# One block of loads re-cut for the DMA engines, first stores held back, first pair turned early: a weight-normalised matrix product on one Trainium2 core

## Chip, cores, metric

One core of a Trainium2 chip. The metric is the device time of one execution in microseconds; times are medians of several runs. A run is "fast" or "slow" by its time against the fastest run of the same kernel; comparisons use fast runs. A ratio below is the mean time of one kernel's fast runs over the mean of the other's of the same rounds, so it is not quite the ratio of the medians that stand beside it.

## The reference

```python
W_adapted = W + scale * (lora_A @ lora_B)                       # 256 x 256
W_norm = np.sqrt(np.sum(W_adapted ** 2, axis=0, keepdims=True) + 1e-8)
W_final = W_adapted / W_norm * m
y = x.reshape(-1, 256) @ W_final                                # 32768 x 256, float32
```

Nearly all bytes are x (33.6 MB in) and y (33.6 MB out).

## The kernel before

x comes in eight blocks of 4096 rows. A block lies in SBUF as 128 partitions of 32 KB, one contiguous stretch of DRAM for each partition. There are five block buffers; y is written over x in the same buffer and stored from there, so the load of block 5 waits for the store of block 0, and so on. A block is eight chunks, two chunks are a pair. For each pair GpSimd rounds x to bf16, TensorE turns it (transposes), VectorE copies it out of PSUM, TensorE multiplies, ScalarE copies the product back.

```python
def load_x(n):
    nc.sync.dma_start(out=in_sbuf(*parts[n]), in_=in_dram(x_flat, *parts[n])
    ).then_inc(sem(f"load{n}"), 16)

def store_y(n):
    nc.scalar.dma_start(out=in_dram(out_flat, *parts[n]), in_=in_sbuf(*parts[n])
    ).then_inc(sem(f"store{n}"), 16)
# ... lora_A, lora_B, m on ScalarE's queue; W and all of x on SyncE's
for n in range(len(parts)):
    b = parts[n][0] // CH
    if b >= XBUFS and parts[n][0] % CH == 0:
        nc.sync.wait_ge(sem(f"store{b - XBUFS}"), 16)
    load_x(n)
# ... ScalarE, after chunk g
    n = part_of[g]
    if g == NCH - 1 or part_of[g + 1] != n:      # the block's last chunk
        nc.scalar.drain().then_inc(sem("done"), 1)
        nc.scalar.wait_ge(sem("done"), n + 1)
        store_y(n)
# ... TensorE
    nc.tensor.wait_ge(dv, 8)                     # the weights are ready
    nc.tensor.sem_inc(sem("room"), 2)
    turned(0)
    with nc.Fori(0, NPR // 2, 1, engines=[PE], head_slot={PE: 128}):
        turned(1)
        product(0)
        product(1)
        turned(0)
```

Of the kernel before, what the change touches and what calls it, by code (L numbers as in the profile page):

```python
# [11 lines left out]
def kernel(  # L12
# [10 lines left out]
    nc = tc.nc  # L23
    P = 128
# [5 lines left out]
    x_flat = x.flatten_outer_dims()  # L30
    out_flat = out.flatten_outer_dims()
    N, IN = x_flat.shape
    OUT = W.shape[1]
    R = lora_A.shape[1]
    KC = IN // P
    J = 4
    DJ = 32
    BLK = DJ * P
    NBLK = N // BLK
# [3 lines left out]
    XBUFS = 5  # L43
    CH = DJ // J
    NCH = NBLK * CH

    NPR = NCH // 2
    PRB = CH // 2
    NXB = 2
    NXT = 2  # L50
    F8 = 2 * J * P

# [7 lines left out]
    def sb(name, shape, dtype):  # L60
        return ctx.enter_context(nc.sbuf_tensor(name, shape, dtype))
# [4 lines left out]
    x_bufs = [sb(f"x_sb{k}", [P, DJ, IN], FP32) for k in range(XBUFS)]  # L66
    xb_bufs = [sb(f"xb{k}", [P, 2 * J, IN], BF16) for k in range(NXB)]
    xt_bufs = [sb(f"xt{k}", [P, F8, KC], BF16) for k in range(NXT)]
    w_nat = sb("w_nat", [P, KC, OUT], FP32)
    a_nat = sb("a_nat", [P, KC, R], FP32)  # L70
    b_nat = sb("b_nat", [R, OUT], FP32)
# [28 lines left out]
    def sem(name):  # L100
        if name not in sems:
            sems[name] = tc.alloc_semaphore(name)
        return sems[name]
# [1 line left out]



    parts = [(b * CH, CH) for b in range(NBLK - 1)]
    parts += [(NCH - CH, CH // 2), (NCH - CH // 2, CH // 2)]
    part_of = {}  # L110
    for n, (g0, cnt) in enumerate(parts):
        for g in range(g0, g0 + cnt):
            part_of[g] = n

    def in_sbuf(g0, cnt):
        b, c = divmod(g0, CH)
        return x_bufs[b % XBUFS][:, c * J : (c + cnt) * J, :]

    def in_dram(dram, g0, cnt):
        return dram[g0 * J * P : (g0 + cnt) * J * P].rearrange("(p j) k -> p j k", p=P)  # L120

    def load_x(n):
        nc.sync.dma_start(
            out=in_sbuf(*parts[n]), in_=in_dram(x_flat, *parts[n])
        ).then_inc(sem(f"load{n}"), 16)

    def store_y(n):
        nc.scalar.dma_start(
            out=in_dram(out_flat, *parts[n]), in_=in_sbuf(*parts[n])
        ).then_inc(sem(f"store{n}"), 16)  # L130


# [1 line left out]
        out=w_nat[:], in_=W.rearrange("(p t) o -> p t o", t=KC)  # L134
    ).then_inc(sem("load_w"), 16)
    nc.scalar.dma_start(
        out=a_nat[:], in_=lora_A.rearrange("(p t) r -> p t r", t=KC)
    ).then_inc(sem("load_a"), 16)
    nc.scalar.dma_start(out=b_nat[:], in_=lora_B).then_inc(sem("load_b"), 16)
    nc.scalar.dma_start(out=m_row[:], in_=m[None, :]).then_inc(sem("load_m"), 16)  # L140
    for n in range(len(parts)):
        b = parts[n][0] // CH
        if b >= XBUFS and parts[n][0] % CH == 0:
            nc.sync.wait_ge(sem(f"store{b - XBUFS}"), 16)
        load_x(n)


    nc.gpsimd.memset(zeros[:], 0.0).then_inc(sem("pool"), 1)
    nc.gpsimd.wait_ge(sem("pool"), 1)
    nc.gpsimd.affine_select(  # L150
        out=identity[:],
        in_=zeros[:],
# [5 lines left out]
    ).then_inc(sem("ident"), 1)  # L158
    for p in range(NPR):
        b, c = divmod(p, PRB)  # L160
        if p == 0 or part_of[2 * p - 1] != part_of[2 * p]:
            nc.gpsimd.wait_ge(sem(f"load{part_of[2 * p]}"), 16)
        if p >= NXB:
            nc.gpsimd.wait_ge(sem("turned"), p - NXB + 1)
        nc.gpsimd.tensor_copy(  # L165
            out=xb_bufs[p % NXB][:],
            in_=x_bufs[b % XBUFS][:, 2 * c * J : 2 * (c + 1) * J, :],
        ).then_inc(sem("rounded"), 1)

    nc.gpsimd.wait_ge(sem("turned"), NPR - NXB + 1)  # L170
    nc.gpsimd.memset(xb_bufs[NPR % NXB][:], 0.0).then_inc(sem("rounded"), 1)  # L171


    dv = sem("dve")
    nc.vector.memset(ones[:], 1.0)
    nc.vector.memset(eps_col[:], 1e-8).then_inc(dv, 1)
    nc.vector.wait_ge(sem("load_b"), 16)
    nc.vector.tensor_copy(out=b_bf[:], in_=b_nat[:])  # L178
    nc.vector.wait_ge(sem("pe"), 1)
    nc.vector.tensor_copy(out=aT[:], in_=aT_ps).then_inc(dv, 1)  # L180
# [3 lines left out]
        out=wa[:], in0=ab_ps, scalar=float(scale), in1=w_nat[:], op0=ALU.mult, op1=ALU.add  # L184
# [15 lines left out]
    for p in range(NPR):  # L200
        nc.vector.wait_ge(sem("turned"), p + 1)
        nc.vector.tensor_copy(  # L202
            out=xt_bufs[p % NXT][:].rearrange("p r t -> p (r t)").bitcast(FP32),
            in_=xt_ps[p % 2][:],
# [8 lines left out]
        out=norm[:], in_=n2_ps, func=AF.Sqrt, bias=eps_col[:]  # L213
    ).then_inc(sem("act"), 1)
    for g in range(NCH):
        b, c = divmod(g, CH)
        nc.scalar.wait_ge(sem("product"), g + 1)

        nc.scalar.copy(  # L219
            out=x_bufs[b % XBUFS][:, c * J : (c + 1) * J, :], in_=y_ps[g % 2][:]  # L220
        ).then_inc(sem("room"), 1)
        n = part_of[g]
        if g == NCH - 1 or part_of[g + 1] != n:
            nc.scalar.drain().then_inc(sem("done"), 1)
            nc.scalar.wait_ge(sem("done"), n + 1)
            store_y(n)


    pe = sem("pe")
# [17 lines left out]
    i.then_inc(pe, 1)  # L247
    nc.tensor.wait_ge(sem("load_m"), 16)
    nc.tensor.matmul(mb_ps, ones[0:1, :], m_row[:], start=True, stop=True).then_inc(pe, 1)  # L249

    nc.tensor.wait_ge(dv, 8)
    nc.tensor.sem_inc(sem("room"), 2)

    def take(name):

        nc.tensor.sem_inc(sem(name), -1).wait_op(sem(name), 1, "sem-ge")  # L256
# [6 lines left out]
    def turned(p):  # L263
        take("rounded")

        for j in range(2 * J):
            i = nc.tensor.transpose(  # L267
                xt_ps[p % 2][:, j * P : (j + 1) * P],
                xb_bufs[p % NXB][:, j, :].bitcast(FP32),
                identity[:],  # L270
            )
        i.then_inc(sem("turned"), 1)

    def product(p):
        take("copied")
        for h in range(2):
            take("room")
            for t in range(KC):
                for j in j_order:
                    r = (h * J + j) * P  # L280
                    i = nc.tensor.matmul(  # L281
                        y_ps[h][:, j, :],
                        xt_bufs[p % NXT][:, r : r + P, t],
                        w_final[:, t, :],
                        start=(t == 0 and (j % (J // 2)) == 0),
                        stop=(t == KC - 1 and (j % (J // 2)) == (J // 2) - 1),
                    )
            i.then_inc(sem("product"), 1)

    turned(0)  # L290
    with nc.Fori(0, NPR // 2, 1, engines=[PE], head_slot={PE: 128}):
        turned(1)
        product(0)
        product(1)
        turned(0)


    critical.close()
# [40 lines left out]
```

## Time and profile before

| | before |
|---|---|
| median of the first three runs | 164.03 us (163.66 to 164.14) |
| span of the profiled run | 163.2 us |
| share of the 16 DMA engines, both queues | 96.8% |
| busiest compute engine (TensorE) | 65% |
| end of the last packet: 15 engines / the last engine | 159.5 to 160.3 / 162.69 us |

Two kinds of reading occur below. Views of the profile give shares and GB/s of a stretch; they count a packet where it starts, so a short stretch is rough. The packet records of the trace give start, duration, size and queue of every DMA packet, but no engine number; a packet often starts within 3 to 4 ns of the end of another, and such a row of packets (a lane) is read as one engine's. A "count" is one of the 16 landings that the trace has for a DMA's semaphore, read as one for each engine (block 0 of the kernel before: 13.50 to 13.78 us; its last store: 159.84 to 163.16 us). "Lost" time is what a stretch of packets falls short of 433 GB/s, the rate from 60 to 137 us of the kernel before. The lines themselves stand in the prediction.

### The profile page before, as it was taken

The numbers are of one execution on the slowest core, as the hardware profiler recorded it, in microseconds if no ns is written. First come the engines' busy times: TensorE is split into PE (matmuls) and PEld (weight loads), VectorE is DVE, ScalarE is ACT, GpSimd is POOL, SyncE is SP. The second block draws the span as 40 slices with busy tenths as digits, with TensorE's granted clock in tenths as the row PEclk, the third lists the DMA queues.
The fourth block names the chain that finished last, engine by engine and source line by source line (L and its number), as shares of the span: only waits on it lengthen the run. The fifth ranks groups of instructions, "written<-read, shape, count | busy, mean of one in ns | idle before, by whom it ended". The sixth has DMA issues, their size and how long they took to land. (4 is left out here: it accounts for less than half of the span.)

```text
span 163.2 us, 1988 instructions
## 1 busy us (share of the span) xinstructions
PE 105.3 (65%) x786; PEld 85.2 (52%) x786; DVE 47.2 (29%) x44; ACT 63.8 (39%) x67; POOL 62.5 (38%) x39
## 2 busy tenths in 40 slices
PE   1270599789789897898981998619988820892000
PEld 0130577677577775776760867418676610771000
DVE  0429452350532514405230325005051400330000
ACT  3010027548366384473754053900738440062000
POOL 1006381753935738268004940069209003900000
PEclk9999999999999999999998589985899996599755
DMA  5998998998999999999999999999999999998991
GB/s 201 402 498 386 426 474 385 482 418 265 466 426 426 442 410 466 426 394 482 418 426 442 420 426 458 402 458 410 446 414 454 414 446 422 450 442 377 442 430 60
DMA packets 2915, 67.41 MB, mean 413 GB/s; under 512 B 465, under 2 KB 482, under 8 KB 610
## 3 DMA queue, kind: packets, MB, share of 16 engines
q1 hardware_dynamic: 1440, 33.82, 49.0%
q10 hardware_dynamic: 1474, 33.59, 47.8%
q14 instruction: 1, 0.01, 0.0%
HBM read 33.85 MB, written 33.55 MB: 413 GB/s over the span
## 5 line engine op out<-in xcount | busy, mean ns | idle before, releaser
L219 ACT COPY x_sb<-y_ps 128x1024 f32<-128x1024 f32 x64 | 61.9, 1014 | 75.8 <-PE y_ps L281 75.8
L165 POOL CAST xb<-x_sb 128x2048 bf16<-128x2048 f32 x32 | 60.0, 1902 | 79.3 <-DMA x_sb<-in_x_dram 56.0
L281 PE MATMUL y_ps<-w_final,xt 128*128 128x256 bf16 x512 | 64.6, 280 | 12.8 <-PEq L256 12.8
L202 DVE COPY xt<-xt_ps 128x1024 f32<-128x1024 f32 x32 | 38.2, 1221 | 88.1 <-PE xt_ps L267 88.0
L281 PEld LDWEIGHTS y_ps<-w_final,xt 128*128 128x128 bf16 x512 | 48.4, 100 | 28.2 <-issue 19.8
L267 PE MATMUL xt_ps<-identity,xb 128*128 128x128 f32 x264 | 39.1, 309 | 23.1 <-PEq L256 23.1
L267 PEld LDWEIGHTS xt_ps<-identity,xb 128*128 128x128 f32 x264 | 34.9, 161 | 25.8 <-issue 25.6
L198 DVE TENSOR_TENSOR w_final<-wam,rnorm 128x256 bf16<-128x256 f32 x2 | 4.0, 2028 | 0.0
L244 PE MATMUL y_ps<-sq,ones 128*128 128x256 f32 x4 | 2.1, 674 | 1.6 <-DVE sq L187 1.6
L233 PE MATMUL y_ps<-identity,a_nat 128*16 128x128 f32 x2 | 0.6, 397 | 3.6 <-DMA a_nat<-in_lora_A_dram 3.6
L212 ACT ACTIVATE norm<-y_ps,eps_col 128x256 f32<-128x256 f32 x1 | 0.5, 473 | 6.1 <-PE y_ps L244 6.1
L244 PEld LDWEIGHTS y_ps<-sq,ones 128*128 128x128 f32 x4 | 1.2, 323 | 2.3 <-DVE sq L187 2.1
L210 ACT ACT_TABLE_LOAD x1 | 1.3, 1283 | 2.4 <-issue 2.4
L233 PEld LDWEIGHTS y_ps<-identity,a_nat 128*16 128x16 f32 x2 | 0.1, 90 | 3.6 <-issue 3.6
L171 POOL MEMSET xb<- 128x2048 bf16 x1 | 1.8, 1805 | 0.3 <-PE xt_ps L267 0.3
L195 DVE RECIPROCAL rnorm<-norm 128x256 f32<-128x256 f32 x1 | 1.7, 1745 | 0.0
L237 PE MATMUL y_ps<-b_bf,aT 16*128 16x256 bf16 x2 | 0.6, 404 | 1.5 <-DVE aT L180 1.5
L189 DVE COPY m_all<-y_ps 128x256 f32<-128x256 f32 x1 | 0.4, 425 | 3.3 <-PE y_ps L249 3.3
L178 DVE CAST b_bf<-b_nat 16x256 bf16<-16x256 f32 x1 | 0.3, 281 | 3.8 <-DMA b_nat<-in_lora_B_dram 3.8
L249 PE MATMUL y_ps<-m_row,ones 1*128 1x256 f32 x2 | 1.2, 710 | 0.0
L237 PEld LDWEIGHTS y_ps<-b_bf,aT 16*128 16x128 bf16 x2 | 0.1, 106 | 1.9 <-DVE aT L180 1.9
L183 DVE SCALAR_TENSOR_TENSOR wa<-y_ps,w_nat 128x512 f32<-128x512 f32 x1 | 0.7, 692 | 0.8 <-PE y_ps L237 0.8
(13 smaller groups left out, 3.7 us busy)
## 6 DMA issues: line engine op xcount, KB each, us to landing
x_sb<-in_x_dram SPq DMA_DIRECT2D x7, 4096.0 KB, 27.1
out_dram<-x_sb ACTq DMA_DIRECT2D x7, 4096.0 KB, 37.2
x_sb<-in_x_dram SPq DMA_DIRECT2D x2, 2048.0 KB, 29.6
out_dram<-x_sb ACTq DMA_DIRECT2D x2, 2048.0 KB, 20.2
w_nat<-in_W_dram SPq DMA_DIRECT2D x1, 256.0 KB, 2.9
a_nat<-in_lora_A_dram ACTq DMA_DIRECT2D x1, 16.0 KB, 2.6
b_nat<-in_lora_B_dram ACTq DMA_DIRECT2D x1, 16.0 KB, 3.6
m_row<-in_m_dram ACTq DMA_DIRECT2D x1, 1.0 KB
```

Source lines behind the costliest of these rows:

```text
L165: nc.gpsimd.tensor_copy(out=xb_bufs[p % NXB][:], in_=x_bufs[b % XBUFS][:, 2 * c * J : 2 * (c + 1) * J, :],).then_inc(sem("rounded"), 1)
L171: nc.gpsimd.memset(xb_bufs[NPR % NXB][:], 0.0).then_inc(sem("rounded"), 1)
L183: nc.vector.scalar_tensor_tensor(out=wa[:], in0=ab_ps, scalar=float(scale), in1=w_nat[:], op0=ALU.mult, op1=ALU.add).then_inc(dv, 1)
L195: nc.vector.reciprocal(out=rnorm[:], in_=norm[:]).then_inc(dv, 1)
L198: i = nc.vector.tensor_mul(out=w_final[:, t], in0=wam[:, t], in1=rnorm[:])
L202: nc.vector.tensor_copy(out=xt_bufs[p % NXT][:].rearrange("p r t -> p (r t)").bitcast(FP32), in_=xt_ps[p % 2][:],).then_inc(sem("copied"), 1)
L210: nc.scalar.activation(out=warm[:], in_=eps_col[:], func=AF.Sqrt)
L219: nc.scalar.copy(out=x_bufs[b % XBUFS][:, c * J : (c + 1) * J, :], in_=y_ps[g % 2][:]).then_inc(sem("room"), 1)
L244: i = nc.tensor.matmul(n2_ps, ones[:], sq[:, t, :], start=(t == 0), stop=(t == KC - 1))
L249: nc.tensor.matmul(mb_ps, ones[0:1, :], m_row[:], start=True, stop=True).then_inc(pe, 1)
L267: i = nc.tensor.transpose(xt_ps[p % 2][:, j * P : (j + 1) * P], xb_bufs[p % NXB][:, j, :].bitcast(FP32), identity[:],)
L281: i = nc.tensor.matmul(y_ps[h][:, j, :], xt_bufs[p % NXT][:, r : r + P, t], w_final[:, t, :], start=(t == 0 and (j % (J // 2)) == 0), stop ...
```

## The change

The intent: one DMA engine ends its last store some 2.5 us after the others. 60 KB of its share of block 1 are to go to the other 15, by loading 30 partitions on GpSimd's queue so that one engine gets none of them. Also: stores start later (chunk 13 instead of 7), the first pair is loaded and turned before the weights are ready, and TensorE takes turning and multiplying by turns.

```diff
+    HOLD = 13
+    loads = [(0, 2), (2, CH - 2)] + [(b * CH, CH) for b in range(1, NBLK - 1)]
+    issue = [max(g0 + cnt - 1, HOLD + n) for n, (g0, cnt) in enumerate(stores)]
...
+    SLOW = 5
+    SIDE = 30
+    def side_loads():                         # GpSimd's queue, before identity is made
+        by_gpsimd(b_nat[0 : SLOW + 1], lora_B[0 : SLOW + 1], "load_b0", OUT * 2)
+        by_gpsimd(dst[0:SIDE], src[0:SIDE], "side", half)          # dst: block 1
+        by_gpsimd(b_nat[SLOW + 1 : R], lora_B[SLOW + 1 : R], "load_b1", OUT * 2)
...
+        if n == n_side:
+            for p0 in range(SIDE, 32):        # rows 30 and 31, in pieces of 1 KB
+                for s in range(2):
+                    nc.sync.dma_start(
+                        out=dst[p0 : p0 + 1].rearrange("p (j s) k -> p s j k", s=2)[:, s],
+                        in_=src[p0 : p0 + 1].rearrange("p (j s) k -> p s j k", s=2)[:, s],
+                    ).then_inc(sem(f"rows{p0}_{s}"), 16)
+            p0 = 32
+        nc.sync.dma_start(out=dst[p0:P], in_=src[p0:P]).then_inc(sem(f"load{n}"), 16)
...
-    nc.scalar.dma_start(out=b_nat[:], in_=lora_B).then_inc(sem("load_b"), 16)
...
+        if p == 0:
+            nc.gpsimd.wait_ge(sem("dve"), 4)
...
-    nc.tensor.wait_ge(dv, 8)
-    nc.tensor.sem_inc(sem("room"), 2)
     turned(0)
+    nc.tensor.wait_ge(dv, 8)
+    nc.tensor.sem_inc(sem("room"), 2)
     with nc.Fori(0, NPR // 2, 1, engines=[PE], head_slot={PE: 128}):
         turned(1)
         product(0)
+        turned(0)
         product(1)
-        turned(0)
```

More of the change, by code (lines that the diff above doesn't have):

```diff
@@ L103, in sem @@
         return sems[name]
-    parts = [(b * CH, CH) for b in range(NBLK - 1)]
-    parts += [(NCH - CH, CH // 2), (NCH - CH // 2, CH // 2)]
-    part_of = {}
-    for n, (g0, cnt) in enumerate(parts):
-        for g in range(g0, g0 + cnt):
-            part_of[g] = n
+    loads = [(0, 2), (2, CH - 2)] + [(b * CH, CH) for b in range(1, NBLK - 1)]
+    loads += [(NCH - CH, CH // 2), (NCH - CH // 2, CH // 2)]
+    load_of = {g: n for n, (g0, cnt) in enumerate(loads) for g in range(g0, g0 + cnt)}
+    stores = [(b * CH, CH) for b in range(NBLK - 1)]
+    stores += [(NCH - CH, CH // 2), (NCH - CH // 2, CH // 2)]
+    issue = [max(g0 + cnt - 1, HOLD + n) for n, (g0, cnt) in enumerate(stores)]
     def in_sbuf(g0, cnt):
@@ L119, in in_dram, with by_gpsimd, wait_x @@
     def in_dram(dram, g0, cnt):
+        if g0 + cnt <= CH:
+            block = dram[0:BLK].rearrange("(p j) k -> p j k", p=P)
+            return block[:, g0 * J : (g0 + cnt) * J, :]
         return dram[g0 * J * P : (g0 + cnt) * J * P].rearrange("(p j) k -> p j k", p=P)
-    def load_x(n):
-        nc.sync.dma_start(
-            out=in_sbuf(*parts[n]), in_=in_dram(x_flat, *parts[n])
-        ).then_inc(sem(f"load{n}"), 16)
+    SLOW = 5
+    SIDE = 30
+    n_side = next(n for n, (g0, _) in enumerate(loads) if g0 == CH)
+    assert loads[n_side] == (CH, CH)
+    def by_gpsimd(out, in_, name, size):
+        nc.gpsimd.dma_start(
+            out=out, in_=in_, max_dma_last_dim=size, single_packet=True
+        ).then_inc(sem(name), 16)
+    def side_loads():
+        dst, src = in_sbuf(CH, CH), in_dram(x_flat, CH, CH)
+        half = DJ * IN * 2
+        by_gpsimd(b_nat[0 : SLOW + 1], lora_B[0 : SLOW + 1], "load_b0", OUT * 2)
+        by_gpsimd(dst[0:SIDE], src[0:SIDE], "side", half)
+        by_gpsimd(b_nat[SLOW + 1 : R], lora_B[SLOW + 1 : R], "load_b1", OUT * 2)
+    def load_x(n):
+        dst, src = in_sbuf(*loads[n]), in_dram(x_flat, *loads[n])
+        p0 = 0
+        if n == n_side:
[7 more added lines that the diff above has]
+        nc.sync.dma_start(out=dst[p0:P], in_=src[p0:P]).then_inc(sem(f"load{n}"), 16)
+    def wait_x(n):
+        nc.gpsimd.wait_ge(sem(f"load{n}"), 16)
+        if n == n_side:
+            nc.gpsimd.wait_ge(sem("side"), 16)
+            for p0 in range(SIDE, 32):
+                for s in range(2):
+                    nc.gpsimd.wait_ge(sem(f"rows{p0}_{s}"), 16)
     def store_y(n):
         nc.scalar.dma_start(
-            out=in_dram(out_flat, *parts[n]), in_=in_sbuf(*parts[n])
+            out=in_dram(out_flat, *stores[n]), in_=in_sbuf(*stores[n])
         ).then_inc(sem(f"store{n}"), 16)
@@ L138 @@
     ).then_inc(sem("load_a"), 16)
-    nc.scalar.dma_start(out=b_nat[:], in_=lora_B).then_inc(sem("load_b"), 16)
     nc.scalar.dma_start(out=m_row[:], in_=m[None, :]).then_inc(sem("load_m"), 16)
-    for n in range(len(parts)):
-        b = parts[n][0] // CH
-        if b >= XBUFS and parts[n][0] % CH == 0:
+    for n in range(len(loads)):
+        b = loads[n][0] // CH
+        if b >= XBUFS and loads[n][0] % CH == 0:
             nc.sync.wait_ge(sem(f"store{b - XBUFS}"), 16)
         load_x(n)
+    side_loads()
     nc.gpsimd.memset(zeros[:], 0.0).then_inc(sem("pool"), 1)
@@ L160 @@
         b, c = divmod(p, PRB)
-        if p == 0 or part_of[2 * p - 1] != part_of[2 * p]:
-            nc.gpsimd.wait_ge(sem(f"load{part_of[2 * p]}"), 16)
+        if p == 0 or load_of[2 * p - 1] != load_of[2 * p]:
+            wait_x(load_of[2 * p])
+        if p == 0:
+            nc.gpsimd.wait_ge(sem("dve"), 4)
         if p >= NXB:
@@ L176 @@
     nc.vector.memset(eps_col[:], 1e-8).then_inc(dv, 1)
-    nc.vector.wait_ge(sem("load_b"), 16)
+    nc.vector.wait_ge(sem("load_b0"), 16)
+    nc.vector.wait_ge(sem("load_b1"), 16)
     nc.vector.tensor_copy(out=b_bf[:], in_=b_nat[:])
@@ L221 @@
         ).then_inc(sem("room"), 1)
-        n = part_of[g]
-        if g == NCH - 1 or part_of[g + 1] != n:
-            nc.scalar.drain().then_inc(sem("done"), 1)
-            nc.scalar.wait_ge(sem("done"), n + 1)
-            store_y(n)
+        for n in range(len(stores)):
+            if issue[n] == g:
+                nc.scalar.drain().then_inc(sem("done"), 1)
+                nc.scalar.wait_ge(sem("done"), n + 1)
+                store_y(n)
     pe = sem("pe")
```

## The prediction

> **What bounds the kernel now.** I read the page from the top: engine shares, the 40 slices, the DMA queues, the chain; then the queue's own waits, the stretches, and last the packet records of the trace, because the page alone does not say what the 16 DMA engines lose.
>
> ```profile
> span 163.2 us, 1988 instructions
> PE 105.3 (65%) x786; PEld 85.2 (52%) x786; DVE 47.2 (29%) x44; ACT 63.8 (39%) x67; POOL 62.5 (38%) x39
> ...
> DMA  5998998998999999999999999999999999998991
> GB/s 201 402 498 386 426 474 385 482 418 265 466 426 426 442 410 466 426 394 482 418 426 442 420 426 458 402 458 410 446 414 454 414 446 422 450 442 377 442 430 60
> ...
> q1 hardware_dynamic: 1440, 33.82, 49.0%
> q10 hardware_dynamic: 1474, 33.59, 47.8%
> ...
> ACT 1%; PE 1%; issue 0%
> ```
>
> No compute engine is above 65%, and the chain of compute that ended last covers 2% of the span: it stops at 148.1 us, 15 us before the end. The two hardware queues (q1 loads, q10 stores) fill 96.8% of the 16 DMA engines. So the bound is DMA, and the question is only where the remaining 3% is. The stretches show it:
>
> ```profile
> core 0: us, PE busy (x) PEld busy (x) DVE busy (x) ACT busy (x) POOL busy (x), PEclk, DMA share, GB/s
> 0.00:4.00 4.00, 0.36 (x2) 0.12 (x2) 0.17 (x2) 1.49 (x2) 0.70 (x6) 1.00 0.54 205
> ...
> 36.00:40.00 4.00, 3.68 (x34) 3.00 (x33) 0.63 (x1) 2.83 (x3) 2.04 (x2) 1.00 1.12 344
> ...
> 60.00:137.00 77.00, 56.24 (x431) 45.74 (x428) 21.48 (x18) 35.74 (x37) 29.89 (x16) 0.91 1.01 433
> ...
> 160.00:163.20 3.20, 0.00 (x0) 0.00 (x0) 0.00 (x0) 0.00 (x0) 0.00 (x0) 0.50 0.05 20
> ```
>
> From 60 to 137 us the engines run full at 433 GB/s. (A stretch bins a packet by its start, so shares over 1 are rounding.) There are three losses: the first 3 us; a dip at 36 to 40 us; and the last 3 us, where 20 GB/s is less than the 27 GB/s (433/16) of one engine.
>
> The packet records resolve the last two. A 32 KB packet takes 1.213 us, and an engine's share is 8 partitions x 8 blocks x 2 directions = 128 of them, 155.3 us. Big packets start at 3.05 us. The dip is 31 load packets of 1.35 to 2.9 us just after the first store was issued at 34.5 us; integrated against 433 GB/s it costs each engine 1.3 us. 3.2 + 155.3 + 1.3 = 159.8, and indeed 15 engines end their last packet between 159.5 and 160.3 us. One ends at 162.69; its last count lands at 163.16. That engine is about 2.9 us late. In loads, all 16 counts of blocks 0 to 2 land within 0.3 us of each other; every later store has one count some 2.5 to 3 us behind the median. Among the store packets 47 took a mean of 1.258 instead of 1.213 us, which adds up to 2.1 us and is spread evenly from 40 us on, about one engine's worth. So one engine is slower in stores, and it alone sets the last 2.4 us (162.69 less 160.3).
>
> Stores also gate later loads:
>
> ```profile
> SPq L123 <- DMA out_dram<-x_sb: 95.5, 3, 56.8
> ```
>
> This looks like the largest wait, but costs nothing: while SyncE waits for a buffer, earlier stores and loads are queued and the engines stay full.
>
> [...]loads and stores together never exceed the 433 GB/s that loads alone have. [...]w_final's two products took 2028 ns each beside GpSimd casts at 13.8 to 17.8 us, wam's two of the same size 0.76 us together. That explains why the new first cast waits until DVE has squared the weights.
>
> **The change part by part.**
>
> *Side load.* Of block 1, partitions 0 to 29 leave SyncE's queue: 960 KB over 15 engines, 64 KB each. Partitions 32 to 127 stay, 6 per engine, 192 KB. Rows 30 and 31 are cut into four DMAs of 16 pieces of 1 KB, 4 KB per engine. So 15 engines carry 260 instead of 256 KB, and the chosen one 196, 60 KB less. At 1.213 us per 32 KB: the chosen one gains 2.2 us, the others lose 0.15. If the chosen one is the late one, its end goes from 162.69 to 160.5, and the others' latest from 160.3 to 160.5[...]. Plus 0.47 to the landing: a span near 161.2, 2.0 less. The timed median exceeds the span by 164.03 - 163.2 = 0.83: 162.0 timed.
>
> *lora_B on GpSimd, identity after it.* b_nat landed at about 5.0 us. Now its second part queues[...] behind 64 KB of side load (2.4 us alone, more while sharing), and three DMA issues come before the identity (1.7 us before, perhaps 4 to 5 now). I take weights chain entry at 7 to 8 us; from b_nat's cast at 5.0 to w_final's end at 18.0 it took 13 us, so weights at 20 to 21.
>
> *First pair ahead.* PE's first eight transposes (18.3 to 20.3 us) go in front of the wait for w_final: that takes back about 2 us. First product stays at 21 to 23 us (before 21.8). All of this is off the bound: loads of five blocks keep the engines busy for 3.2 + 5 x 9.7 = 51.7 us without any store.
>
> *First store held to chunk 13.* Two pairs take 6.6 us in the timeline, 1.65 per chunk. Before, chunk 7 ended at 34.4; chunk 13 thus comes near 44, some 8 us before the load queue would run dry. Work is neither removed nor added. The dip should move from 36 to about 46 us and keep its size: in it some 0.56 MB are missing, 35 KB per engine, about one packet[...]. The worth is 0 if so, up to 1.3 if the dip depends on when it happens.
>
> *TensorE by turns.* It fills the 0.69 and 0.32 us gaps per two pairs. PE's waits are not on the bound: the last load lands at 137, the last store is issued at 148.2, and the preceding stores keep the engines busy until 158.3. Worth 0.
>
> Sum: -2.0 (side load), 0 (the rest), and a quarter of 1.3 for a dip that may vanish, -0.2 to -0.3: 164.03 - 2.0 - 0.2 = 161.8.
>
> **The rivals.**
>
> 1. The slow engine is not the skipped one[...]. Then the late engine gets 4 KB more: 164.2. For it: no number in the records, nothing before that uses this queue. Against it: the change is written for exactly one number, and the lateness is consistent from 58 us to the end.
>
> 2. The dip vanishes with the hold[...]. Then all engines gain 1.3 more: about 160.6, over 2% faster. For it: someone chose 13, a place that otherwise buys nothing. Against: the deficit has the size of one packet per engine.
>
> 3. GpSimd's queue costs more than counted[...]. The other 15 engines then set the end, at 161 to 161.5: 162.5 to 163. A worse form, weights so late that chunk 13 comes after 52 us and the engines run dry, needs weights 8 us later than I estimate; I give it 3%.
>
> **Range and chances.** Most likely 161.8. Low end 160.4: balance perfect and the dip gone. High end 163.8: slow engine only partly relieved. Beyond it lies rival 1, about 10%. Faster by over 2% means under 160.75, which needs nearly all of the dip's 1.3 us: 20%. Slower by over 2% means above 167.3, only by the engines running dry: 2%.
>
> **What would show it.** Span near 161; in the last store, the last count within about 0.5 us of the others instead of 2.6; last slices full to within 1 us of the end; a dip of about 1.3 us near 44 to 48 us instead of 36 to 40; loads-only rate of 433 GB/s until then; w_final at 20 to 21 us; first store issued near 44. Wrong if the late count remains 2 to 3 us behind (rival 1), if the dip is absent or larger (rival 2), or if a slice other than these is below 430 GB/s (rival 3).

An allowance of 0.2 us in the side-load step had no measurement behind it. That the chosen engine is left out, and that it is the late one, were assumptions. The sum included the allowance: 160.5 + 0.2 + 0.47 gave the span near 161.2, which is the -2.0, and 164.03 - 2.0 - 0.2 = 161.8.

## The result, and the profile after

The changed kernel takes 178.04 us (176.87 to 180.01, 4 runs) against 164.05 (4 runs): ratio 1.0834, 95% interval 1.0774 to 1.0894. It is 8% slower, where the prediction said 160.4 to 163.8. Its profiled run, 180.01 us, is the slowest of the four; the spans of the three fast ones are 175.3, 176.1 and 176.8 us against its 178.4. The reading below rests on a loss of some 13 to 14 us, which the fast runs show too (176.87 to 178.35 us), not on that difference.

The page after: the row of GB/s shows where the time went.

```profile
span 178.4 us, 1999 instructions
...
DMA  5999997998999999999999899899998999999993
GB/s 184 347 209 222 280 205 169 213 235 375 448 463 404 426 463 404 426 463 426 404 455 463 375 455 463 382 450 415 415 492 386 463 419 452 411 433 452 393 428 147
...
q1 hardware_dynamic: 1680, 32.83, 51.3%
q10 hardware_dynamic: 1442, 33.57, 43.7%
q0 software_dynamic: 144, 1.00, 2.6%
```

The seven slices from about 9 to 40 us move 169 to 280 GB/s, although the DMA row says that the engines are busy there. Busy and moving half: each packet takes longer (1.99 times in the median from 26 to 40 us). The queue that was meant to do the trick, q0, takes just 2.6% of the engines; the load queue q1 takes 51.3% for fewer bytes than before (32.83 instead of 33.82 MB at 49.0%).

The stretches after (window, its length, busy us of each engine with instructions, granted TensorE clock, DMA share, GB/s):

```profile
4.00:7.00 3.00, 0.59 (x2) 0.10 (x2) 0.00 (x0) 0.00 (x0) 0.16 (x1) 1.00 1.19 453
7.00:20.00 13.00, 0.00 (x0) 0.00 (x0) 0.00 (x0) 0.00 (x0) 0.00 (x0) 1.00 0.99 213
20.00:26.00 6.00, 0.00 (x0) 0.00 (x0) 0.00 (x0) 0.00 (x0) 0.00 (x0) 1.00 1.07 222
26.00:41.00 15.00, 8.34 (x29) 5.70 (x30) 8.13 (x12) 0.47 (x1) 6.22 (x4) 1.00 1.00 227
41.00:63.00 22.00, 22.00 (x201) 20.37 (x200) 10.22 (x9) 15.61 (x17) 15.57 (x9) 1.00 1.01 433
63.00:150.00 87.00, 58.24 (x486) 51.94 (x484) 24.66 (x21) 40.48 (x42) 34.66 (x19) 0.87 1.00 429
```

From 7 to 41 us half rate at full occupation, before and after it the old 433. By the packet records the losses are 6.6 us from 7 to 20 (the side load runs beside the second piece of block 0), 2.8 from 20 to 26 (the 1 KB pieces of rows 30 and 31) and 7.6 from 26 to 42 us (partitions 32 to 127 of block 1: 94 packets of 32 KB start between 26 and 40 us, and their median takes 1.99 times its time at 27 GB/s). The sum is 17.0. The dip of 1.3 us at the first store is missing in this run, and the last engine is 2.4 instead of 2.9 us late: 17.0 - 1.3 - 0.5 = 15.2 = 178.4 - 163.2.

The waits after show a second thing that was far off, the second part of lora_B:

```profile
DVE b_bf L226 <- DMA b_nat<-in_lora_B_dram: 26.0, 1, 26.0
...
PE y_ps L281 <- POOL identity L193: 4.2, 1, 4.2
```

It landed at 27.1 us; VectorE idled 26 us for it, w_final was finished at 37.7 us and the first store issued at 59.6. None of this set the end: the engines did not run dry, because the five blocks of loads, slowed, lasted beyond 63 us.

### The profile page after: what moved, and what is told of

Read it like the earlier page. It is cut to its first block, busy times and chain, and to the rows that moved or that the text cites. A ratio compares the mean times of both kernels' runs of the same rounds, so it can differ in the third digit from the quotient of the medians.

```text
span 178.4 us, 1999 instructions
## 1 busy us (share of the span) xinstructions
PE 98.7 (55%) x786; PEld 86.5 (48%) x786; DVE 45.6 (26%) x44; ACT 63.8 (36%) x67; POOL 64.5 (36%) x42
## 3 DMA queue, kind: packets, MB, share of 16 engines
q1 hardware_dynamic: 1680, 32.83, 51.3%
## 5 line engine op out<-in xcount | busy, mean ns | idle before, releaser
L250 DVE COPY xt<-xt_ps 128x1024 f32<-128x1024 f32 x32 | 39.2, 1224 | 84.0 <-PE xt_ps L311 84.0
L325 PEld LDWEIGHTS y_ps<-w_final,xt 128*128 128x128 bf16 x512 | 52.4, 102 | 7.5
L311 PEld LDWEIGHTS xt_ps<-identity,xb 128*128 128x128 f32 x264 | 33.1, 153 | 39.0 <-issue 38.6
L137 POOL DMA_DIRECT2D b_nat<-in_lora_B_dram x2 | 1.2, 623 | 1.1 <-SPq L59 1.1
L246 DVE TENSOR_TENSOR w_final<-wam,rnorm 128x256 bf16<-128x256 f32 x2 | 1.5, 796 | 0.0
```

The costliest lines, as they stand in the source:

```text
L137: nc.gpsimd.dma_start(out=out, in_=in_, max_dma_last_dim=size, single_packet=True).then_inc(sem(name), 16)
L246: i = nc.vector.tensor_mul(out=w_final[:, t], in0=wam[:, t], in1=rnorm[:])
L250: nc.vector.tensor_copy(out=xt_bufs[p % NXT][:].rearrange("p r t -> p (r t)").bitcast(FP32), in_=xt_ps[p % 2][:],).then_inc(sem("copied"), 1)
L311: i = nc.tensor.transpose(xt_ps[p % 2][:, j * P : (j + 1) * P], xb_bufs[p % NXB][:, j, :].bitcast(FP32), identity[:],)
L325: i = nc.tensor.matmul(y_ps[h][:, j, :], xt_bufs[p % NXT][:, r : r + P, t], w_final[:, t, :], start=(t == 0 and (j % (J // 2)) == 0), stop ...
```

## The experiments

**Theory P:** the pieces into which block 1 is cut make DMA engines collide by the partitions that they write at the same time, so their packets take twice as long (by the records after, 1.99 times 1.213 us in the median). Which partitions collide was the author's assumption; the numbers that P forecasts in e5, e11, e13 and e14 rest on it, no run shows it as a rule. **Rivals:** the late weights and held stores (W), TensorE's order and the split first load (T), GpSimd's queue as such (G), addresses in DRAM (D), an engine slow by itself at partitions other than those that a 128-row load gives it, assumed too (E), any DMA that is not 128 rows (S or M). Loads of 128 rows run at full rate: 437 GB/s from 4 to 34 us of the kernel before, 434 from 4 to 36 us of e1.

All runs but e3 and e4 are e1 with the edit shown (lines marked + and - are against the changed kernel; e4's is against the kernel before). e1 to e7 were timed in three rounds; the others are single looks of unknown state, used for packet durations only. Packet durations are given as multiples of 1.213 us, the time of a 32 KB packet.

### e1_no_side: everything but the side load

```diff
-    side_loads()
+    nc.scalar.dma_start(out=b_nat[:], in_=lora_B).then_inc(sem("load_b"), 16)
     # block 1: one DMA of 128 partitions on SyncE, no rows, no piece of 96
```

> Everything of the change but the side load: block 1 is one 128-partition load on SyncE again, lora_B comes on ScalarE's queue, the split first load, the first pair ahead, the hold and the turns stay. Theory P (the pieces of block 1 make the DMA engines collide, so that packets take twice their 1.21 us between 6.5 and 41 us): all of the loss goes, loads run at 433 GB/s from 4 us on, 162.5 to 164.2 us timed, the last count still 2.5 to 3 us behind. Rival W (late weights and the held stores cost the time): still over 170 us. Rival T (the other order on TensorE or the split first load cost it): over 170 us.

Measured: 164.02 us against 163.71, ratio 1.0033 (1.0001 to 1.0066). The stretch at the start:

```profile
4.00:36.00 32.00, 26.03 (x185) 21.42 (x186) 15.40 (x18) 12.54 (x14) 17.79 (x10) 1.00 1.01 434
```

The whole loss is gone with the side load and the cut of block 1. The rest of the change (hold, first pair ahead, turns, split load) is worth nothing, as predicted. T falls, and of W the held stores. The late weights are not tested here, since lora_B is back on ScalarE's queue and comes early; e2, where it comes early too (VectorE waits 3.0 us for it), still loses most of the time. The last count of the last store is 2.0 us behind the median.

### e2_split_hw: the cut without GpSimd's queue

```diff
+        if n == n_side:
+            nc.sync.dma_start(out=dst[0:32], in_=src[0:32]).then_inc(sem("side"), 16)
+            p0 = 32
         nc.sync.dma_start(out=dst[p0:P], in_=src[p0:P]).then_inc(sem(f"load{n}"), 16)
```

> As e1, but block 1 is loaded as two DMAs of SyncE's queue, partitions 0 to 31 and 32 to 127; nothing on GpSimd's queue. Theory P, shape half: both pieces run at about 216 GB/s (packets 2.4 us), so 4 MB take 19.4 instead of 9.7 us: 8 to 10 us over e1, 171 to 174 us, a half-rate stretch of about 19 us. Rival G (only GpSimd's queue disturbs the engines, the shape is harmless): equal to e1 within 1 us, packets of 1.21 us.

Measured: 172.97 us, ratio 1.0605 (1.0545 to 1.0666), 8.95 us over e1.

```profile
4.00:13.00 9.00, 6.23 (x18) 3.37 (x17) 4.58 (x8) 0.47 (x1) 1.89 (x1) 1.00 1.04 439
14.00:33.00 19.00, 10.59 (x72) 9.01 (x72) 4.96 (x5) 5.89 (x6) 5.62 (x3) 0.97 0.98 221
34.00:48.00 14.00, 12.37 (x100) 11.33 (x101) 4.90 (x4) 6.87 (x8) 10.89 (x6) 0.84 0.99 426
```

The same 4 MB, the same queue, the same rows, only cut at partition 32: half rate for 19 us, packets at 1.8 to 2.1. So the shape alone does it, and G does not hold as the sole cause. The records' loss is 9.8 us; here too the dip is missing, which makes up the difference to 8.95.

### e3_side_full: GpSimd's side load, then block 1 in one piece

```diff
         p0 = 0
         if n == n_side:
-            ...                               # rows 30, 31; p0 = 32
+            nc.sync.wait_ge(sem("side"), 16)
```

> GpSimd's queue as in the changed kernel (6 partitions of lora_B, 30 partitions of block 1, 10 partitions of lora_B); then, once that has landed, SyncE loads the whole block 1 with 128 partitions, so no rows of 1 KB and no 96-partition piece; the 0.96 MB are loaded twice (2.2 us of the engines). Theory P: half rate while the side load lasts (7 to about 20 us: 13 us at 213 GB/s, 6.6 us lost of which 2.2 are the extra bytes), full rate after it; 168 to 172 us. Rival S (the 96-partition piece alone is at fault): full rate beside the side load, e1 plus 2 to 3 us. Also: which lane of packets has no side-load packet, and whether it is the one with the 1.26 us stores.

Measured: 170.55 us, ratio 1.0461 (1.0394 to 1.0528), 6.5 over e1, of which 2.3 are the bytes loaded twice.

```profile
4.00:6.00 2.00, 0.60 (x2) 0.10 (x2) 0.00 (x0) 0.00 (x0) 0.15 (x1) 1.00 1.25 527
7.00:17.00 10.00, 0.00 (x0) 0.00 (x0) 0.00 (x0) 0.00 (x0) 0.00 (x0) 1.00 1.00 268
18.00:50.00 32.00, 24.99 (x168) 20.77 (x169) 14.84 (x17) 11.67 (x13) 16.98 (x9) 1.00 1.00 429
```

Ten us at 60% of the rate beside the side load, full rate after it; the records' loss is 4.2 us. So the side load is harmful by itself too, and rival S of this run (only the piece of 96) falls. (The letter S stands for other rivals in e13 and e14.)

This run also answers for whom the side load was made. One lane has no 16 KB packet on q0: it is the spared engine, ahead of the others in each load (its counts are written at 28.88, 38.56 and 48.25 us, the next lane's at 29.20, 38.91 and 48.62). Followed to the stores, its packets from 61.17 us on take 1.213 us (from 57.5 us on two lanes have the same times, but both show 1.213). The lane whose stores take 1.27 to 1.31 us in that stretch, traced back, holds four side-load packets. **The spared engine was not the late one.** The changed kernel agrees: the last count of its last store is 2.4 us behind the median (178.39 against 175.97 us), no less than in e1, where no engine was spared.

### e4_hold_only and e7_hold19: the hold

```diff
+    HOLD = 13                                 # e4: the kernel before, nothing else changed
-    HOLD = 13
+    HOLD = 19                                 # e7: e1 with a longer hold
```

> The kernel before with the hold alone: the first store is issued after chunk 13 instead of 7, about 44 instead of 34.5 us. My prediction: the dip of 1.3 us moves to about 46 us and keeps its size: 164.0 us. The rival of the prediction: the dip goes, 162.7 us. In the changed kernel no dip was seen when stores began at 62 us.

> e1 with the first store after chunk 19 instead of 13, about 45 to 46 instead of 37.5 us, still before the load queue runs dry near 52. If the dip after the first store has a fixed size (about 1 us in e1 and e4): equal to e1. If it goes when stores begin later, as in the runs where they began at 49 to 60 us: 1 us less than e1.

Measured: e4 163.80 us, ratio 1.0008 (0.9979 to 1.0037); e7 163.50 us, ratio 0.9993 (0.9933 to 1.0054). The dip moved with the first store and lost 1.1 us in e4 (43 to 50 us) and 0.9 in e7 (46 to 53), against 1.3 before and 1.0 in e1. The hold neither costs nor gains, in either place.

### e5_stride3: pieces of every third row

```diff
+            for s in range(3):
+                nc.sync.dma_start(out=dst[s : 96 : 3], in_=src[s : 96 : 3]
+                ).then_inc(sem(f"side{s}"), 16)
+            p0 = 96
```

> As e2, but block 1 is loaded as three DMAs of 32 partitions each with a step of three (0, 3, 6, ... 93; then 1, 4, ...; then 2, 5, ...) and one of partitions 96 to 127. Each 32-row piece gives two rows to each of 16 engines as the 32-row piece of e2 did[...]. Theory P[...]: the three stepped pieces run at 1.2 to 1.5 times 1.21 us on average, some packets at 1.0 and some at 2.0; only the last piece is at 2.0; 3 to 6 us over e1. Rival M (the row order in the DRAM source, or any DMA that is not 128 rows, halves the rate): all pieces at 2.0 as in e2, 9 us over e1.

Measured: 172.03 us, ratio 1.0512 (1.0448 to 1.0576). After the first round of packets the stepped pieces ran at 1.87 to 1.99, no packet at 1.0. The forecast of P, as I had worked it out, failed, and the rival's number was nearly met. What followed had to tell whether partitions matter at all.

### e6_rows_only: the 1 KB pieces alone

```diff
+            for r in range(SIDE, 32):         # rows 30, 31 into a buffer loaded later
+                for s in range(2):
+                    nc.sync.dma_start(out=spare[r : r + 1]..., in_=src[r : r + 1]...)
```

> e1 plus the four DMAs of 1 KB pieces of rows 30 and 31 alone (into the same partitions of a buffer that is loaded later, after a wait), the rest of block 1 whole. 64 KB more, 0.15 us of the engines. Theory P: [...]64 KB at 27 GB/s take 2.4 us: 1.5 to 2.5 us over e1. Rival: hidden, e1 plus 0.2 us.

Measured: 164.83 us against 163.78, ratio 1.0051 (1.0002 to 1.01); 0.8 over e1 in another set of rounds, under the 1.5 that P expected. P's 2.4 us were an estimate, 64 KB at the rate of one engine (433/16). The records show a loss of 1.9 us at 13 to 17 us, as expected, but the dip at the first store is missing, and the two nearly offset. The stretch:

```profile
13.00:17.00 4.00, 0.00 (x0) 0.00 (x0) 1.95 (x4) 0.00 (x0) 1.63 (x1) 1.00 1.13 278
```

### e9_src4 and e10_near_rows: DRAM or SBUF

```diff
+                nc.sync.dma_start(out=dst[32*s : 32*s + 32], in_=src[s : P : 4])...    # e9
+            steps[0][0] //= 2                 # e10: 128 rows, 16 KB apart in DRAM
+            src = bass.AP(tensor=src.tensor, offset=src.offset, ap=steps)
```

Their outputs are wrong, which doesn't matter for the times.

> Wrong result on purpose. [...]Block 1 as four DMAs of 32 partitions in a row each, as in e2's first piece, but the rows read from DRAM are four apart[...]. Theory D (addresses in DRAM make the packets slow): 1.0 to 1.2 times 1.21 us. Theory P[...] and theory E[...]: 2.0, as in e2.

> Wrong result on purpose. Block 1 as one 128-partition DMA, whose rows in DRAM are 16 KB apart instead of 32 (they overlap)[...]. Theory D: slow, near 2.0. Theories P and E: 1.0.

Measured: e9 1.96 to 2.12 in all pieces after the first round; e10 1.0 in all packets of block 1. The stretches of e9, then of e10:

```profile
14.00:32.00 18.00, 10.97 (x72) 9.38 (x72) 4.74 (x4) 5.88 (x6) 5.63 (x3) 1.00 0.99 204
```

```profile
14.00:32.00 18.00, 16.18 (x122) 14.44 (x123) 7.11 (x6) 8.67 (x9) 12.73 (x7) 1.00 1.01 437
```

Rows four apart in DRAM are as slow as neighbours; rows 16 KB apart are at full rate if the DMA has 128 partitions. For these spacings DRAM is out (D); it is the SBUF side or the shape.

### e11_eight: partitions under 64, from 64 on, and seven rows of the first again

```diff
+            for h in range(4):
+                for r in range(4):
+                    a = 32 * h + r            # 8 rows, four partitions apart
+                    nc.sync.dma_start(out=dst[a : a + 29 : 4], in_=src[a : a + 29 : 4])...
+            for r in range(4):                # 7 rows, from the second of them on
+                nc.sync.dma_start(out=x_bufs[4][4+r : 29+r : 4], in_=src[4+r : 29+r : 4])...
```

> Block 1 as 16 DMAs of 8 partitions with a step of four: 0, 4, ... 28 and so on; each has one row for each of engines 0 to 7[...]. Then partitions 64 to 127[...]. Then four DMAs of 7 partitions (4, 8, ... 28) on engines 0 to 6, into a spare buffer[...]. Theory P: first part 1.0, second about 2.0 for both groups of engines, third 1.0. Theory E: first part 1.0, second 2.0 for engines 0 to 7 and 1.0 for the others, third 2.0. Theory D: 1.0 in all[...]. The total says nothing: engines 0 to 7 carry all of block 1, 165 to 185 us.

The engine numbers in this text are the author's, as the records carry none; the "first part" is the eight DMAs of partitions under 64. Measured by the landings of successive DMAs. The first eight land 1.21 to 1.43 us apart, the first five 1.21 to 1.22. The next eight (partitions from 64 on, while the other engines load block 2) land 2.45 to 2.57 us apart, and the packets of both groups take 2.0 to 2.1 (some at the end 1.8):

```profile
25.00:42.00 17.00, 0.37 (x4) 0.09 (x1) 0.00 (x0) 1.46 (x2) 0.00 (x0) 0.62 1.02 214
```

The four of 7 rows land 1.2 to 1.3 us apart (median count), except one engine of the seven with 2.3 to 2.5 us; why that one, no record shows. So E falls: it expected the packets of the other group at 1.0 and the seven rows at 2.0. Block 2, at full rate in e1, is slowed beside partitions from 64 on, and they beside it: here two groups of engines halve each other.

### e8_probe and e12_probe2: which engine is late

```diff
+    for k in range(16):
+        wide, rows = 16 * (k + 1), 3 if k == 8 else 2
+        nc.gpsimd.dma_start(out=probe[0:rows, at : at + wide], in_=lora_B[0:rows, 0:wide])...
         # e12: the same with single_packet and a capped row length
```

> e1 plus 16 tiny loads on GpSimd's queue of 2 or 3 rows, each of its own size, so that the packets of an engine name it by two sizes. No difference in time to speak of. It shows which engine is the one with the slow stores; the side load spared the engine that had no 16 KB packet in e3, and that was not the slow one there (which had four of them, and a 1 KB packet of the second lora_B load[...]).

> e8 again, where all 16 tiny loads put their rows on the same two engines and so named nothing; now with the two options that the side load has (single packet, capped row length)[...]. Expected: successive pairs of engines, and the engine with the slow stores named by its two sizes[...].

e8 named nothing: two lanes took two rows of every one of the 16 loads. In e12 the first five loads (64 to 320 bytes) still share one pair of lanes; from the sixth on they moved to others. The lane with the slow stores holds packets of 384 and of 896 bytes, but the same trail also holds a packet of 832 bytes, so that two sizes do not name it; several lanes lay too close in time. Which engine is late stays open.

### e13_sixteen and e14_fifteen: partitions or the shape

```diff
+                    rows = slice(s, s + 15 * step + 1, step)   # e13: 16 rows, step 7, then 4
+                    rows = slice(s, s + 14 * 9 + 1, 9)         # e14: 15 rows, step 9
+                    nc.sync.dma_start(out=spare[rows], in_=src[rows])...
```

> e1 plus six DMAs of 16 partitions, one row for each engine (so no order of rows within an engine to assume), 3 MB more into buffers that are loaded later: first three with a step of seven[...], then three with a step of four[...]. Theory P: with step seven about 12 of 16 packets at 1.0 times 1.21 us and 4 near 2.0; with step four all near 2.0. Rival S (every DMA that is spread over 16 engines and is not 128 rows runs at half rate): all near 2.0 in both. 9 us over e1 at most, of which 7.3 are the extra bytes at full rate if it were so.

> e1 plus four DMAs of 15 partitions with a step of nine (0, 9, ... 126, then 1, 10, ... 127, each into two spare buffers)[...]. [...](theory P, with whatever makes the whole DMA slow down in e13): 13 or 14 of 15 packets at 1.0 times 1.21 us. If any DMA of 15 or 16 rows that is not 128 rows is slow (rival S): all near 1.75 to 2.1.

Measured: e13, step seven: after the first few packets 1.74 to 1.8, all engines nearly alike; step four: 2.07 to 2.1. e14, 15 rows with step nine: 1.0 to 1.2 for all but two lanes, those two at 2.0 to 2.2. P had expected one or two slow packets of 15; which two engines the lanes are, no record says. The stretches of e13 (step seven, then step four), then of e14:

```profile
14.00:19.00 5.00, 2.91 (x14) 2.57 (x15) 1.97 (x2) 0.00 (x0) 4.64 (x3) 1.00 0.87 210
19.00:27.00 8.00, 6.77 (x60) 5.92 (x58) 2.74 (x3) 5.78 (x6) 1.00 (x1) 1.00 1.02 213
```

```profile
13.00:23.00 10.00, 6.99 (x39) 5.95 (x40) 3.65 (x6) 2.02 (x2) 5.63 (x3) 1.00 1.03 393
```

15 rows are not 128, and they run at 1.0 to 1.2 on all but two lanes: rival S falls in the form that e14 gave it. With e11 this shows that a DMA of other than 128 rows can run at full rate (e14; partitions under 64 of e11, 1.21 to 1.43 us apart) or at half, and that engines at work at the same time can halve each other (both groups of e11 at 2.0 to 2.1). Which partitions make the difference is not shown. Nor does it settle the whole loss. In e2, e5 and e13 all 16 packets of a round take nearly the same time (e13, step seven: 1.74 to 1.8; the 96 partitions of e2: rounds at 1.85 to 1.92 and at 2.1 by turns), also those that P, as worked out for e5 and e13, expected at 1.0. In e11 (the 7 rows) and e14 one or two slow lanes slowed nobody else. No run shows why.

So a rival stands, S as e13 put it: any DMA spread over all 16 engines with other than 128 rows is slow. It forecast nearly 2.0 for step seven too, where 1.74 to 1.8 was measured; but every large DMA of that kind here was slow, and e14 has 15 rows. No run had 16 rows of which P expected 1.0 throughout. That the cut into pieces costs the time is shown; that partitions written at the same time explain all of it is not.

No experiment pointed to a version that beats both kernels: e1, e4 and e7 equal the kernel before, and freeing one engine by such a side load leaves a remainder of about a hundred partitions, which was slow in e2. A split like that of e14, 15 rows on 15 engines at nearly full rate (393 GB/s from 13 to 23 us), was not tried for this.

## Why the prediction was wrong, point by point

- **What bounds the kernel** held: DMA engines, with losses at the start, at the dip and at one late engine. e1, e4 and e7 confirm it from the other side: changes to compute and to the time of the first store moved nothing.
- **The side-load step failed, twice.** First, its size: it took every 32 KB packet at 1.213 us whoever carries it, and allowed 0.2 us more without a measurement. In fact the engines moved half their rate beside the side load (213 GB/s from 7 to 20 us), and packets of the 96-partition remainder took about twice 1.213 us: 17.0 us lost in all by the records. e2 shows the remainder with the 32-partition piece (9.8 lost; from landings the 96 took 14.4 us, the 32 about 5), e3 the side load (4.2), e6 the rows (1.9). The parts do not add up to 17.0 exactly: 7.1 for the 96 (14.4 less the 7.3 of 3 MB at full rate), 4.2 and 1.9 make 13.2; the rest, 3.8, may be what they do to each other when in flight together; that was not tried.
- Second, its condition, "if the chosen one is the late one". e3 shows that it was not. Even without collisions the late engine would have kept its lateness: the prediction had this as its first rival, with 10%.
- **Rival 3** (GpSimd's queue costs more) pointed nearest, but gave 162.5 to 163 and looked at the wrong object: it asked about the queue, where the cut of block 1 mattered (e2, without that queue, lost 8.95 us).
- **lora_B** was put at 7 to 8 us and landed at 27.1, as its second part waited behind slowed side-load packets (its packets start at 17.84 to 21.75 us, the last of the side load at 18.29); w_final came at 37.7 instead of 20 to 21, the first store at 59.6 instead of 44. The claim that this is off the bound held, though by luck: loads at full rate would have run dry near 52 us (the prediction's estimate, 3.2 + 5 x 9.7), before a first store at 59.6; only because they were slow too did they last.
- **Hold, first pair ahead, turns** were each put at 0: right (e1 1.0033, e4 1.0008). The dip was said to move and to keep its size: right in e4 and e7. It is missing in the changed kernel, in e2 and in e6, runs in which engines had collided before the first store, and small (0.4 us) in e3; why was not tried.
- **The signs to look for** worked: a slice below 430 GB/s outside the known places was named as the mark of rival 3, and the row of GB/s showed it at once.
- **Two slips in its figures** change nothing: a quarter of 1.3 is 0.33, not 0.2 to 0.3; and the records hold 25 load packets of 1.35 to 2.9 us in the dip, not 31. The loss of 1.3 us there is right.

## What to carry to other kernels

When DMA is the bound, look at how the transfers are cut by partitions and what is in flight beside them, not only at how many bytes and engines they have: a block cut into 32 and 96 partitions loaded at half the rate of the same block in one DMA of 128 (221 GB/s from 14 to 33 us of e2, 434 from 4 to 36 us of e1). Here a cut by columns was harmless where the cut by partitions was not (the first load of two chunks, 128 partitions of 8 KB, ran at nearly full rate: 0.309 us for 114 of its 128 packets of 8 KB after). And before moving work off a slow engine, show which engine it is.
